# Hybrid decoder step: stick-breaking heads ahead of the delta rule, and paged attention of the samples in plain float32 on four column groups

## The chip, the cores and the metric

The kernel runs on one core of one Trainium2 chip. The metric is device microseconds of a whole execution; the figure given for a kernel is the median of its runs. Engines: PE (TensorE), DVE (VectorE), ACT (ScalarE), POOL (GpSimd), SP (which issues most DMAs).

## The reference

One layer of a decoder trunk runs for two groups with the same weights: a prompt of 512 tokens, and 8 samples of 4 new tokens each, which have 512 past tokens in a paged key and value cache (4 pages of 128 tokens per sample). Per layer:

```
h = RMSNorm(x);  one projection h @ w_in gives  sq,sk,sv | gq,gk,gv,ga,gb,gz
SB, 8 heads of 128:   z = q.k * scale + bias;  w = sigmoid(z) * prod over later keys of (1 - sigmoid(z'));  o = w @ v
                      (samples: keys and values are the cached pages and the 4 new rows)
GDN, 8 heads of 128:  short causal convolution (4 taps) and silu on q|k|v, then the gated delta rule
                      S <- g*S + k (v - w S)^T  in chunks of 64 tokens, o = q S + ...;  o = RMSNorm(o) * silu(gz)
x += [o_SB | o_GDN] @ w_out
x += w_xo @ cross attention(RMSNorm(x), 256 memory tokens, 4 heads, QK-norm, softmax)
x += SwiGLU(RMSNorm(x))
```

Besides the two outputs, new keys and values, the GDN states (8 samples x 8 heads x 128 x 128, and the prompt's), the convolution's last rows and the memory's keys and values are returned. All of it is float32.

## The kernel before, in words

Activations lie transposed, features on the 128 partitions and the 544 tokens (512 + 32) in two halves of 272. A dense product of float32 accuracy is made of three fp32r products of high and low parts: `products` issues six matmuls (`wh,ah`, `wh,al`, `wl,ah`, two halves each) for one 128x128 block of weights. `project` makes one head's 128 output features out of 16 such blocks; `w_in` alone is 64 projects, `mix_out` 16 more. Weights arrive as 512 KB tiles and are split by ACT (`wh`) and DVE (`wl`).

Everything that is not a dense product is *side work*, written as Python generators: a head (`sb_head`, `gdn_head`), the samples' part of four heads (`sb_sample`, `gdn_sample`), `conv_state`. The class `Side` holds two queues of them, `hi` for heads and `lo` for samples. After each group of six dense matmuls `products` calls `tick(0.68)`, which adds 0.68 times `ratio` to a credit; while there is credit, the next generator that is not pausing is run to its next `yield cost, latency`. The cost is taken off the credit, and the generator pauses until the planned time has moved on by the latency. `limits` tells how many of each queue may be open at once. `finish` and `drain` force steps whatever the credit. All of it happens when the program is built: what comes out is a fixed order on every engine, which a scheduler of the tile framework may still move a little. So costs, latencies, ratio and queue order decide what stands beside what on PE.

The order of the stages is: load of x with the first two projections (GDN's q and k of head 0), raw v, constants, then eight GDN heads at ratio 0.8, with `gdn_sample` of four heads each put in the low queue after heads 3 and 7, then `conv_state`; eight SB heads at ratio 2, with `sb_sample` after heads 3 and 7; eight gate heads (`gate_head`, projecting gz); `w_out`; cross attention; SwiGLU. In the trace GDN heads go from about 52 to 480 us, SB heads to about 900, gate heads to about 1093, `w_out` to about 1330, cross attention to about 1480, SwiGLU to the end.

What the samples do on PE: `sample_logits` takes one unit (a sample, two pages or two heads: a 128x512 tile), transposes its four 128x128 blocks (`transposes`, L970), splits the result into high and low parts (`parts`, ACT L666 and DVE L667), and makes four products of 128x256 against a window `win` (L684, L685) that holds the queries of one sample at its own columns and zeros elsewhere, so that all samples add into one PSUM tile (L709). `sample_values` splits pages of values in the same way and makes, for each page, two products (high and low) with 32 rows out (L760); four samples' results are copied side by side into `os`. The cross attention of samples already takes unsplit pages of values (`split=False`, L1509). `gdn_sample` ends with the new states: for each head and four samples one product with K = 32 rows (L1256), then DVE adds it to the old state times a decay, and DMA takes it back. `invert` transposes a triangular inverse by way of DRAM (`scr` to `T`), after which L915 uses it. On PE a plain float32 matmul shows in the trace as two entries.

Of the kernel before, what the change touches and what calls it, by code (L numbers as in the profile page):

```python
# [15 lines left out]
P = 128  # L16
# [7 lines left out]
NB = 8  # L24
# [51 lines left out]
def build_consts(c):  # L76
# [11 lines left out]
    sel(c.cm, [[1, P]], -1, -1, ALU.is_ge, 0.0)  # L88
    c.neg = ones("neg", [P, P], 0.0, pool=pb)
# [15 lines left out]
    def blk(t, fill=0.0, inner=4):  # L105
        sel(t, [[-4, 32], [0, inner]], 1, 0, ALU.is_ge, fill)
        sel(t, [[4, 32], [0, inner]], -1, 3, ALU.is_ge, fill)
# [7 lines left out]
    c.cm4 = ones("cm4", [P, P], pool=pb)  # L115
    blk(c.cm4)
    sel(c.cm4, [[1, P]], -1, -1, ALU.is_ge, 0.0)
# [4 lines left out]

    c.selw = ones("selz", [P, 192], 0.0, pool=c.pc)
    c.selz = c.selw[:, 64:128]
    for part in range(2):
        sel(c.selz, [[-64, 2], [8, 8], [-1, 4]], 1, -56 - 4 * part, ALU.not_equal, 1.0)

    c.selv = ones("selv", [P, 64], 0.0, pool=c.pc)
    for part in range(2):
        sel(c.selv, [[-4, 4], [-32, 4], [-1, 4]], 1, -16 * part, ALU.not_equal, 1.0)  # L130
# [248 lines left out]
def first_projections(c):  # L379

    nc = c.nc
    w = [[None] * 4 for _ in range(2)]

    def wload(q):
        for i in range(2):
            w[i][q] = weights(c, c.w_in, q * 4, 4, 3072 + i * 1024, eng=nc.scalar if q + i == 0 else None)
# [94 lines left out]
def sb_project(c, h, acts, rstd):  # L481
    nc = c.nc
    raw = []
    for i in range(3):
        ps = project(c, c.w_in, 0, i * 1024 + h * P, acts)
# [99 lines left out]
def sb_sample(c, g):  # L585

    nc = c.nc
    q, k, v = (x[:, g * 4 : g * 4 + 4, :].rearrange("p h t -> p (h t)") for x in c.sbs)
    ps = c.aux()
    for i, x in enumerate((q, k)):  # L590
        sq = c.tt("sq")
        nc.vector.tensor_mul(sq[:, :P], x, x)
        nc.tensor.matmul(ps[:, i * P : (i + 1) * P], c.ones, sq[:, :P], start=True, stop=True)
# [36 lines left out]
    for h2 in range(2):  # L630
# [6 lines left out]
        nc.scalar.copy(zt[:, :512], ps)  # L637
        for p in range(PAGES):
            o = p * P + h2 * 64
            nc.tensor.matmul(psz[:, o : o + 64], zt[:, p * P : (p + 1) * P], c.selz, start=True, stop=True)  # L640
        yield 0.9
# [9 lines left out]
    yield 0.1, 6.0  # L651
# [19 lines left out]
def sample_logits(c, q, h0, load, n, ps=None, col=0):  # L671

    nc = c.nc
    nb, win = 2, []
    for b0 in range(0, NB, nb):
        w = c.tp("win")
        nc.gpsimd.memset(w[:, : nb * 192].bitcast(F32), 0.0)
        for b in range(b0, b0 + nb):  # L680
            o = (b - b0) * 192 + (NB - 1 - b) * 8
            d = w[:, o : o + 256].rearrange("p (h x) -> p h x", h=2)
            x = q[:, h0 * 32 : (h0 + 2) * 32].rearrange("p (h b t) -> p h b t", h=2, b=NB)[:, :, b]
            nc.gpsimd.tensor_copy(d[:, :, 0:4], x)  # L684
            nc.gpsimd.tensor_sub(d[:, :, 4:8], x, d[:, :, 0:4].bitcast(F32))  # L685
            win += [[w[:, (b - b0) * 192 + hh * 64 :][:, :P] for hh in range(2)]]
        yield 0.0, 0.3
    first = ps is None
    if first:
        ps = c.aux()  # L690
# [3 lines left out]
    def ahead():  # L694
        if units:
            nxt.append(parts(c, transposes(c, load(*units.pop(0)))))
# [5 lines left out]
    for u in range(NB * n):  # L702
        b, i = divmod(u, n)
        k2 = nxt.pop(0)
        ahead()
        for hh in range(2):
            for j, k in enumerate(k2):
                o = col + i * 256
                nc.tensor.matmul(  # L709
                    ps[:, o : o + 256], win[b][hh], k.rearrange("p (g h k) -> p h g k", g=2, h=2)[:, hh],  # L710
                    start=first and u == 0 and hh == 0 and j == 0,
                    stop=b == NB - 1 and hh == 1 and j == 1, skip_group_check=True,
                )
        yield 0.9, 0.4
# [3 lines left out]
def sample_values(c, w, n, load, split=True):  # L718
# [7 lines left out]
    for i in range(0, n, 2):  # L726
        t = (c.tp if split else c.tt)("win")
        for j in range(2):
            x = w[:, (i + j) * P : (i + j + 1) * P].rearrange("p (h b t) -> p b h t", h=4, b=NB)
            d = t[:, j * 256 : (j + 1) * 256].rearrange("p (b u h t) -> p b u h t", b=NB, u=2, h=4)  # L730
            nc.scalar.copy(d[:, :, 0], x)
            if split:
                nc.vector.tensor_sub(d[:, :, 1], x, d[:, :, 0].bitcast(F32))
            else:
                nc.gpsimd.memset(d[:, :, 1], 0.0)
        win.append(t)
    yield 0.1
    pso = c.aux()
    units = [(b, i) for b in range(NB) for i in range(n)]
    nxt = []  # L740

    def ahead():
        if units:
            v = load(*units.pop(0))
            nxt.append(parts(c, v) if split else [v])

    ahead()
    ahead()
    ahead()
    yield 0.0  # L750
    for half in range(2):
        o = c.tt("os")
        for b4 in range(4):
            b = half * 4 + b4
            ps = c.aux()
            for i in range(n):
                vs = nxt.pop(0)
                for j, v in enumerate(vs):
                    x = (i % 2) * 256 + b * 32
                    nc.tensor.matmul(ps[:32], win[i // 2][:, x : x + 32], v, start=i == 0 and j == 0, stop=i == n - 1 and j == len(vs) - 1)  # L760
                ahead()
                yield 0.45, 0.4
            nc.scalar.copy(o[b4 * 32 : b4 * 32 + 32, :512], ps[:32])
# [4 lines left out]
        yield 0.9  # L768
# [95 lines left out]
def invert16(c, gt):  # L864
# [33 lines left out]
    yield 0.0, 6  # L898
# [248 lines left out]
def gdn_sample(c, g):  # L1147
# [66 lines left out]
    nc.vector.tensor_copy(qk[:, : 2 * P], pss[:, : 2 * P])  # L1214
    ps = transposes(c, qk, 2)
# [19 lines left out]
    nc.vector.tensor_scalar(on[:, :P], on[:, :P], f, None, ALU.mult)  # L1235
    ps = transposes(c, on, 1)
    o = c.tt("o")
    nc.scalar.activation(o[:, :P], ps[:, :P], AF.Identity, scale=c.g_out)
    nc.sync.dma_start(c.oT[8 + g * 4 : 12 + g * 4, :, NP:].rearrange("h p t -> p h t"), o[:, :P].rearrange("p (h t) -> p h t", h=4))
    yield 0.4  # L1240
# [8 lines left out]
    for hh in range(4):  # L1249
        h = g * 4 + hh  # L1250
        rows = slice(hh * 32, (hh + 1) * 32)
        for w in range(2):
            s = v3(c.load("s1"))
            nc.sync.dma_start(s, c.state[0, w * 4 : w * 4 + 4, h].rearrange("b k d -> k b d"))
            ps = c.aux()
            nc.tensor.matmul(  # L1256
                ps, kn[rows, :], ex[w][rows].rearrange("p b d -> p (b d)"),
                start=True, stop=True, tile_position=(hh * 32, 0),
            )
            for b in range(4):  # L1260
                o = g * 32 + hh * 8 + w * 4 + b
                nc.vector.scalar_tensor_tensor(s[:, b, :], s[:, b, :], c.gend_s[:, o : o + 1], ps[:, b * P : (b + 1) * P], ALU.mult, ALU.add)
            nc.sync.dma_start(c.o_gs_s[0, w * 4 : w * 4 + 4, h].rearrange("b k d -> k b d"), s)
            yield 0.9
# [40 lines left out]
def memory(c):  # L1305
# [22 lines left out]
    for i in range(2):  # L1328
        tiles = [[c.tp("mact") for _ in range(2)] for _ in range(4)]
        acts = [[x[:, k % 2 * 256 : k % 2 * 256 + 256] for x in tiles[k // 2]] for k in range(8)]  # L1330
        for k4 in range(2):
            for a in range(2):
                t = load(i * 2 + k4, a)
                nc.vector.tensor_scalar(t, t, rr[a], None, ALU.mult)
                yield 0.0, 2.0
# [60 lines left out]
def cross_head(c, h, q, out, scale):  # L1396
# [9 lines left out]
    for a2 in range(2):  # L1406
# [5 lines left out]
        yield 0.9, 2.0 * a2  # L1412
# [23 lines left out]
def cross_sample(c, qs, outs, scale, tiles):  # L1436
# [27 lines left out]
    for h2 in range(2):  # L1464
# [13 lines left out]
        ps = yield from sample_logits(c, f, h2 * 2, load, 1, ps if h2 else None, h2 * 256)  # L1478
# [4 lines left out]
    nc.scalar.copy(z[:, :512], ps)  # L1483
    yield 0.0, 1.5
    ps = c.aux()
    for h2 in range(2):
        nc.tensor.matmul(ps[:, :256], c.selw[:, 64 - h2 * 64 :][:, :P], z[:, h2 * 256 : h2 * 256 + 256], start=h2 == 0, stop=h2 == 1)
# [740 lines left out]
def kern(ctx: ExitStack, tc: tile.TileContext, *args, stop=99):  # L2228
# [28 lines left out]
    with tc.tile_pool(name="pb", bufs=1) as pb:  # L2257
# [5 lines left out]
        c.raws = pb.tile([P, 24, 8, 7], F32, name="raws")  # L2263
        c.convp = pb.tile([P, 3, 24], F32, name="convp")
        raws = [gdn_raw(c, i * 8, ps, rstd) for i, ps in enumerate(done)]
        raws.append(gdn_raw(c, 16, project(c, c.w_in, 0, 5120, acts), rstd))
        build_consts(c)
        wc = load_cols(c, "convw", [c.conv_w[0].rearrange("j (m p) -> (j m) p", p=P)], c.pc)
        c.wc = wc.rearrange("p (j m) -> p m j", m=24)
        conv_history(c)  # L2270
# [16 lines left out]
        heads = []  # L2287
        for h in range(8):
            if h > 1:
                side.finish(heads[h - 2], 4)  # L2290
            if h > 2:
                side.finish(heads[h - 3])
            qkv = gdn_project(c, h, acts, rstd) if h else [gdn_conv(c, i * 8, raw) for i, raw in enumerate(raws)]
            if h == 0:
                gates(c, acts, rstd)
            heads.append(side.put(gdn_head(c, h, qkv)))
            if h % 4 == 3:
                side.put(gdn_sample(c, h // 4), True)
        side.put(conv_state(c), True)
        side.limits, side.ratio = (2, 1), 2  # L2300
        for h in range(8):
# [81 lines left out]
```

## Time and profile before

| | us |
|---|---|
| median of 3 runs | 2929.99 (2929.43 to 2930.38) |
| the profiled execution | 2926.94 |
| its span (first to last instruction) | 2925.2 |
| PE busy | 2852.4 |
| mean granted clock of PE | 0.996 |

The profile is of one execution. A row of operations reads: line, engine, operation, output <- inputs, tile (rows*columns of the PE array that the weights take), shape, type, count; behind it the busy time, the mean length of one in ns, and the idle time of the engine ahead of it with what ended it. Matmuls overlap in the pipeline, so the mean length is more than the distance from one start to the next; what a matmul costs is read from starts in the timeline. The waits of an engine are listed by what it waited for. Rows of windows give the length, PE's busy time with its count, the granted clock, the share of DMA and GB/s.

### The profile page before, as it was taken

How to read it: one execution, taken by the hardware profiler on the slowest of the kernel's cores; microseconds unless marked ns; L12 is line 12 of the kernel's file. 1: busy time of each engine (PE TensorE's matmuls, PEld its weight loads, DVE VectorE, ACT ScalarE, POOL GpSimd, SP SyncE). 2: the span in 40 equal slices, each digit the busy share in tenths (PEclk: the TensorE clock that was granted, in tenths of full speed). 3: DMA queues.
4: the chain of work that ended last, by engine and by line, in shares of the span. 5: the costliest groups of instructions: out<-in, count | busy, mean ns of one | idle time of the engine just before them, and what ended most of it. 6: DMA issues, size and time to landing. Idle time of an engine off the chain costs nothing. (4 is left out here: it accounts for less than half of the span.)

```text
span 2925.2 us, 57002 instructions
## 1 busy us (share of the span) xinstructions
PE 2852.4 (98%) x22146; PEld 2762.6 (94%) x22146; DVE 2104.0 (72%) x3320; ACT 1489.1 (51%) x2836; POOL 739.1 (25%) x923
## 2 busy tenths in 40 slices
PE   8999999999999999999989999999999999999998
PEld 7999999889889989999889999999999999999998
DVE  5776775655565565536678888888888887888886
ACT  5544443445555564424654444444444446555675
POOL 3211213312212200003242343333433334221200
PEclk9999999999999999999999999999999999999999
DMA  7323223454463585532544555555455549876653
GB/s 222 92 76 93 79 83 90 132 151 119 131 184 98 177 255 175 149 110 91 166 141 125 173 165 158 155 161 170 146 155 176 154 137 266 262 205 193 196 170 95
DMA packets 633558, 444.39 MB, mean 152 GB/s; under 512 B 36203, under 2 KB 559800, under 8 KB 633288
## 3 DMA queue, kind: packets, MB, share of 16 engines
q1 hardware_dynamic: 601464, 386.31, 44.8%
q0 software_dynamic: 22176, 42.90, 4.8%
q10 hardware_dynamic: 9648, 11.54, 1.1%
q8 instruction: 174, 2.85, 0.4%
q14 instruction: 96, 0.79, 0.1%
HBM read 360.07 MB, written 80.58 MB: 151 GB/s over the span
## 5 line engine op out<-in xcount | busy, mean ns | idle before, releaser
L2030 PE MATMUL gu<-pr,wh 128*128 128x272 f32 x4944 | 672.8, 289 | 7.1 <-ACT pr L1659 3.3
L2030 PEld LDWEIGHTS gu<-pr,wh 128*128 128x128 f32 x4944 | 640.8, 189 | 8.9 <-ACT pr L1659 3.9
L215 PE MATMUL mm<-ah,wh 128*128 128x272 f32 (+1 forms) x2464 | 539.2, 299 | 3.9 <-ACT ah L331 2.8
L215 PE MATMUL mm<-al,wh 128*128 128x272 f32 (+1 forms) x2464 | 525.0, 292 | 0.7 <-DVE al L246 0.7
L215 PE MATMUL mm<-ah,wl 128*128 128x272 f32 (+1 forms) x2464 | 516.5, 290 | 0.1
L1910 PE MATMUL bank<-pr,wh 128*128 128x272 f32 x2464 | 466.1, 289 | 1.1 <-ACT bank L1938 1.1
L215 PEld LDWEIGHTS mm<-ah,wh 128*128 128x128 f32 (+1 forms) x2464 | 392.7, 189 | 26.9 <-issue 8.5
L215 PEld LDWEIGHTS mm<-al,wh 128*128 128x128 f32 (+1 forms) x2464 | 390.3, 189 | 5.4 <-issue 2.0
L215 PEld LDWEIGHTS mm<-ah,wl 128*128 128x128 f32 (+1 forms) x2464 | 387.0, 189 | 2.5 <-DVE wl L204 0.5
L1910 PEld LDWEIGHTS bank<-pr,wh 128*128 128x128 f32 x2464 | 386.3, 189 | 3.1 <-ACT bank L1938 2.9
L204 DVE TENSOR_TENSOR wl<-wr,wh 128x512 fp32r<-128x512 f32 (+1 forms) x340 | 244.6, 724 | 183.2 <-ACT wh L203 174.6
L203 ACT CAST wh<-wr 128x512 fp32r<-128x512 f32 (+1 forms) x340 | 208.3, 615 | 316.4 <-PE mm L215 275.2
L2030 PE MATMUL gu<-pr,wl 128*128 128x272 f32 x2472 | 362.0, 289 | 2.0 <-issue 1.8
L1910 PE MATMUL bank<-pr,wl 128*128 128x272 f32 x1232 | 355.0, 288 | 0.0
L2030 PEld LDWEIGHTS gu<-pr,wl 128*128 128x128 f32 x2472 | 330.4, 189 | 2.4 <-issue 2.0
L1808 DVE TENSOR_TENSOR wl<-sum,wh 128x1024 fp32r<-128x1024 f32 x172 | 221.0, 1285 | 74.9 <-ACT wh L1804 74.9
L1910 PEld LDWEIGHTS bank<-pr,wl 128*128 128x128 f32 x1232 | 232.3, 189 | 0.0
L1804 ACT CAST wh<-sum 128x1024 fp32r<-128x1024 f32 x172 | 180.3, 1048 | 78.2 <-PE gu L2030 41.8
L1808 DVE TENSOR_TENSOR wl<-raw,wh 128x1024 fp32r<-128x1024 f32 x133 | 204.0, 1535 | 15.3 <-ACT wh L1804 13.5
L1804 ACT CAST wh<-raw 128x1024 fp32r<-128x1024 f32 x133 | 140.0, 1052 | 101.2 <-PE gu L2030 95.1
L2095 POOL DMA_DIRECT2D pr<-hT x154 | 81.8, 548 | 255.1 <-PE bank L1910 225.2
L1797 DVE TENSOR_TENSOR sum<-raw,sum 128x1024 f32<-128x1024 f32 x86 | 136.4, 1586 | 0.4
(537 smaller groups left out, 4411.2 us busy)
## 6 DMA issues: line engine op xcount, KB each, us to landing
raw<-in_w_gate_up SPq DMA_DIRECT2D x176, 512.0 KB
wr<-in_w_in SPq DMA_DIRECT2D x108, 512.0 KB
raw<-in_w_down SPq DMA_DIRECT2D x176, 256.0 KB
hT<-hs SPq DMA_DIRECT2D x154, 272.0 KB
pr<-hT POOLq DMA_DIRECT2D x154, 272.0 KB, 6.8
page<-in_cache_sb_k SPq DMA_DIRECT2D x128, 128.0 KB
page<-in_cache_sb_v SPq DMA_DIRECT2D x64, 256.0 KB
wr<-in_w_out SPq DMA_DIRECT2D x32, 512.0 KB
```

The costliest lines, as they stand in the source:

```text
L203: nc.scalar.copy(hi[:, :m, :n], raw[:, k : k + m, :n])
L204: nc.vector.tensor_sub(lo[:, :m, :n], raw[:, k : k + m, :n], hi[:, :m, :n].bitcast(F32))
L215: c.nc.tensor.matmul(ps[:n, h, :HT], l[:, :n], r[:, h * HT : (h + 1) * HT], start=first and i == 0, stop=last and i == 2,)
L1797: self.f.c.nc.vector.tensor_sub(self.a[q], self.a[x], self.a[y])
L1804: self.f.c.nc.scalar.copy(self.hi[q], self.left(q))
L1808: self.f.c.nc.vector.tensor_sub(self.lo[q], self.left(q), self.hi[q].bitcast(F32))
L1910: self.c.nc.tensor.matmul(self.c.bank[bank][:, o], t[x][:, s, i * P : (i + 1) * P], pairs[i].op[q][r], start=new and not (i or n), stop=se ...
L2030: self.c.nc.tensor.matmul(bank, w[:, i * P : (i + 1) * P], self.pairs[i].op[q][r], start=start and n == 0, stop=n == 23, skip_group_check= ...
L2095: self.c.nc.gpsimd.dma_start(t, self.hT[2 * g + pair, :, max(0, 2 * n - 1) + k])
```

## The change

The order of the stages is now: load of x with SB's q and k of head 0; eight SB heads; the gates `gates()`; eight GDN heads; eight gate heads. Ratio is 0.65 for SB and GDN and 2 for gate heads, limits are (2, 1) throughout, and the low queue holds `sb_sample` 0 and 1, `gdn_sample` 0 and 1, `conv_state`. The constants of the delta rule are made after SB head 5. A gate head's product with the GDN output waits in a list until that head is done.

In `sample_logits` the transposed unit is only copied (`kT`), and four plain float32 products of 32 rows out and 128 columns go to the four column groups (one per block of the unit). In `sample_values` pages are used as they are loaded, four samples in four column groups. The logits' re-ordering uses two transposes instead of products with `selz`. In `gdn_sample` two heads' new states are made together, in two row groups, before DVE takes them up. Some yields are new or have longer latencies.

```
 def sample_logits(c, q, h0, load, n, ps=None, col=0):
-        w = c.tp("win") ...                       # windows with high and low parts of q, two samples each
+    w = c.tt("win")
+    nc.gpsimd.memset(w[:, :512], 0.0)
+    for b in range(NB): nc.gpsimd.tensor_copy(win[:, b, :, b * 4 : b * 4 + 4], x)
+    yield 0.0, 3.0
...
-            nxt.append(parts(c, transposes(c, load(*units.pop(0)))))
+            pt = transposes(c, load(*units.pop(0)))
+            k = c.tt("kT")
+            nc.scalar.copy(k[:, :512], pt)
...
-        for hh in range(2):
-            for j, k in enumerate(k2):
-                nc.tensor.matmul(ps[:, o : o + 256], win[b][hh], k..., ...)
-        yield 0.9, 0.4
+        for x in range(4):
+            nc.tensor.matmul(
+                ps[x * 32 : x * 32 + 32, o : o + P], win[:, b, x % 2, :], k[:, x * P : (x + 1) * P],
+                ..., tile_position=(0, x * 32),
+            )
+        yield 0.7, 0.4
 def sample_values(c, w, n, load):
-            nxt.append(parts(c, v) if split else [v])
+    todo = [(half * 4 + b, i) for half in range(2) for i in range(n) for b in range(4)]
+    for _ in range(6): ahead()                    # six pages ahead instead of three
+    yield 0.1, 1.5
...
-                for j, v in enumerate(vs):
-                    nc.tensor.matmul(ps[:32], win[i // 2][:, x : x + 32], v, ...)
-                yield 0.45, 0.4
+            for b in range(4):
+                nc.tensor.matmul(
+                    ps[b * 32 : b * 32 + 32], win[i // 2][:, x : x + 32], nxt[b], ..., tile_position=(0, b * 32),
+                )
+            yield 0.9, 1.0
 def sb_sample(c, g):
+    yield 0.0, 2.0                                # after sq, now one product of 256 columns
-        for p in range(PAGES):
-            nc.tensor.matmul(psz[:, o : o + 64], zt[:, p * P : (p + 1) * P], c.selz, start=True, stop=True)
-        yield 0.9
+        yield 0.0, 1.0
+        for i in range(2):
+            nc.tensor.transpose(out, zt[:, i * P : (i + 1) * P], c.ident)
+        yield 0.25
-    yield 0.1, 6.0
+    yield 0.1, 9.0                                # after run
 invert:       -    yield 0.0, 6     +    yield 0.0, 8       # after the load of T
 gdn_sample:   +    yield 0.0, 1.0 (after qk)   +    yield 0.0, 3.0 (after on)
-    for hh in range(4): for w in range(2): load s; matmul; 4 x DVE; store; yield 0.9
+    for h2 in range(2): for w in range(2): load 2 s; 2 matmuls (row groups hh * 32); 8 x DVE; 2 stores; yield 1.2, 2.0
 memory:       -    yield 0.0, 2.0   +    yield 0.0, 4.0
 cross_head:   -    yield 0.9, 2.0 * a2   +    yield 0.9, 3.5 * a2
 kern:
+        side.limits, side.ratio = (2, 1), 0.65
+        for h in range(8): ... sb_head ...; after h 5 gdn_consts; after h 6 conv_history; after h 3, 7 sb_sample
+        gates(c, acts, rstd)
+        for h in range(8): ... gdn_head ...; after h 3, 7 gdn_sample
+        side.put(conv_state(c), True)
+        side.ratio = 2
+        for h in range(8): ... gate_head ...
```

Three places of the new order. First the values of the pages on PE: before, in `sb_sample` of heads 4 to 7, two products (high and low part of one page) between the six dense ones of a block (`mm`).

```order
L760 MATMUL aux<-part,win 32x512 x2
L215 MATMUL mm<-ah,wh 128x272 x2
L215 MATMUL mm<-al,wh 128x272 x2
L215 MATMUL mm<-ah,wl 128x272 x2
L760 MATMUL aux<-part,win 32x512 x2
```

After, at the start of the values of heads 0 to 3, beside an SB head's own transposes and products (L968, L513):

```order
L752 MATMUL aux<-page,win 32x512 x4
L218 MATMUL mm<-ah,wh 128x272 x2
L218 MATMUL mm<-al,wh 128x272 x2
L218 MATMUL mm<-ah,wl 128x272 x2
L513 MATMUL aux<-part,onesr 128x512 x2
L752 MATMUL aux<-page,win 32x512 x3
L968 MATMUL aux<-ident,raw 128x128 x4
L752 MATMUL aux<-page,win 32x512
L218 MATMUL mm<-ah,wh 128x272 x2
L218 MATMUL mm<-al,wh 128x272 x2
L218 MATMUL mm<-ah,wl 128x272 x2
L752 MATMUL aux<-page,win 32x512 x2
```

A group of four that the code issues together does not stay together: dense products stand between its parts. Over the whole program the 64 products stand in 37 places: 22 of one, 9 of two, 3 of three, 2 of four, 1 of seven.

Second the logits on PE, after: each unit's four products stand in one row, next to the transposes of the unit behind it.

```order
L711 MATMUL aux<-kT,win 32x128 x4
L968 MATMUL aux<-ident,page 128x128 x4
L551 MATMUL aux<-z,sfx 128x128
L711 MATMUL aux<-kT,win 32x128 x4
L968 MATMUL aux<-ident,page 128x128 x4
L218 MATMUL mm<-al,wh 128x272
```

Before, the same place had `L709 MATMUL aux<-part,win 128x256 x4` (or split in two) and the same transposes. Four products of a unit stay four, of half the columns and a quarter of the rows out.

Third POOL in the delta rule, before: `gdn_sample`'s convolution (sqk, sctmp) stands ahead of a head's qd and gt.

```order
L1159 TENSOR_TENSOR sctmp<-raws,convw 128x128
L1161 TENSOR_TENSOR sqk<-sqk,sctmp 128x128
L1065 TENSOR_TENSOR qd<-qd,cv 128x512
L1159 TENSOR_TENSOR sctmp<-raws,convw 128x128
L1161 TENSOR_TENSOR sqk<-sqk,sctmp 128x128
L1159 TENSOR_TENSOR sctmp<-raws,convw 128x128
L1161 TENSOR_TENSOR sqk<-sqk,sctmp 128x128
L1159 TENSOR_TENSOR sctmp<-raws,convw 128x128
L1078 TENSOR_TENSOR gt<-cumrow,sm 128x512
```

After, with the second `gdn_sample`:

```order
L1159 TENSOR_TENSOR sqk<-sqk,sctmp 128x128
L1157 TENSOR_TENSOR sctmp<-raws,convw 128x128
L1063 TENSOR_TENSOR qd<-qd,cv 128x512
L1159 TENSOR_TENSOR sqk<-sqk,sctmp 128x128
L1157 TENSOR_TENSOR sctmp<-raws,convw 128x128
L1159 TENSOR_TENSOR sqk<-sqk,sctmp 128x128
L1076 TENSOR_TENSOR gt<-cumrow,sm 128x512
```

The convolution stays ahead of gt, and the same stands once more with the first `gdn_sample`. On PE the new states (L1256 before, L1259 after) go from 12 places of one and 2 of two to 6 places of two and 1 of four.

More of the change, by code (lines that the diff above doesn't have):

```diff
@@ L121, in build_consts @@
     blk(c.sel4, inner=1)
[L123 to L130, printed above, removed]
     c.id16 = ones("id16", [32, 256], pool=c.pc)
@@ new lines, in sample_values @@
+    for _ in range(6):
+        ahead()
+    yield 0.1, 1.5
+    pso = c.aux()
+    for half in range(2):
+        ps = c.aux()
+        for i in range(n):
+            for b in range(4):
+                x = ((i % 2) * NB + half * 4 + b) * 32
+                nc.tensor.matmul(
+                    ps[b * 32 : b * 32 + 32], win[i // 2][:, x : x + 32], nxt[b], start=i == 0, stop=i == n - 1,
+                    skip_group_check=True, tile_position=(0, b * 32),
+                )
+            del nxt[:4]
+            for _ in range(4):
+                ahead()
+            yield 0.9, 1.0
+        o = c.tt("os")
+        nc.scalar.copy(o[:, :512], ps)
@@ L1486, in cross_sample @@
     for h2 in range(2):
-        nc.tensor.matmul(ps[:, :256], c.selw[:, 64 - h2 * 64 :][:, :P], z[:, h2 * 256 : h2 * 256 + 256], start=h2 == 0, stop=h2 == 1)
+        for k in range(2):
+            nc.tensor.matmul(
+                ps[h2 * 64 : h2 * 64 + 64, k * P : (k + 1) * P], c.ident[:, k * 64 : k * 64 + 64], z[:, h2 * P : (h2 + 1) * P],
+                start=k == 0, stop=k == 1, skip_group_check=True, tile_position=(0, h2 * 64),
+            )
     e = softmax(c, ps, 1)
```

222 lines of the change are left out of this document (107 added, 115 removed).

## The prediction

> **What bounds the kernel now.** I read the page's first part, then the chain of waits, then PE's waits, and last the timeline around the operations that change.
>
> ```profile
> span 2925.2 us, 57002 instructions
> PE 2852.4 (98%) x22146; PEld 2762.6 (94%) x22146; DVE 2104.0 (72%) x3320; ACT 1489.1 (51%) x2836; POOL 739.1 (25%) x923
> 1600.00:2400.00 800.00, 800.00 (x6394) 1.00 0.52 158
> ```
>
> PE is busy for 98% of the span; what is left is 2925.2 - 2852.4 = 73 us. The last row is a window in the SwiGLU part: no idle time at all, 6394 matmuls in 800 us, so a dense slot is 125 ns. Everything after about 1480 us is like this and is not touched. So the time can change in two ways only: PE gets more or less work before 1480 us, or some of the 73 us of waits goes or grows. What the change takes from DVE, ACT or POOL counts only where PE waits for them. The profiled execution took 2926.94 us (1.7 us outside the span), 3.0 us under the median of the runs, 2929.99. I sum against the 2926.94 and add 3 at the end.
>
> PE's waits, by what they were for (us in total, times, longest):
>
> ```profile
> PE aux L312 <- POOL lev L60: 6.4, 1, 6.4
> PE aux L942 <- DVE X L938: 4.1, 1, 4.1
> PE aux L915 <- DMA T<-scr: 3.5, 3, 1.5
> PE aux L1418 <- DVE e L1392: 3.4, 4, 1.6
> PE aux L593 <- DVE sq L592: 2.2, 2, 1.1
> PE aux L709 <- POOL win L685: 2.2, 1, 2.2
> PE aux L654 <- POOL run L650: 1.7, 1, 1.7
> PE aux L970 <- DVE mem L1334: 1.7, 1, 1.7
> PE aux L760 <- DVE part L667: 1.6, 2, 1.0
> PE aux L709 <- POOL win L684: 1.5, 1, 1.5
> PE aux L970 <- DVE qk L1214: 1.0, 1, 1.0
> PE aux L709 <- DVE part L667: 0.9, 2, 0.6
> ```
>
> All but the first two (and L1418) are small waits inside side work: heads or samples whose next step came up on PE before its input was there.
>
> **The change on PE, part by part.** The dense matmuls are the same in number. What changes are the samples' small products, and with them how often PE goes from a full 128x128 product to one in a 32-wide tile and back. Four places of the timeline price that:
>
> ```profile
> 1459.73 1.07 PE L1509 MATMUL aux<-xv,win 128*32 128x512 f32 x8
> 1460.73 0.40 PE L1589 MATMUL mm<-xh,wl 128*128 128x272 f32 x1
> 1460.96 0.29 PE L1589 MATMUL mm<-xh,wh 128*128 128x272 f32 x1
> ...
> 1461.59 0.29 PE L1589 MATMUL mm<-xh,wl 128*128 128x272 f32 x1
> 1461.81 1.18 PE L1509 MATMUL aux<-xv,win 128*32 128x512 f32 x4
> 1462.92 0.40 PE L1589 MATMUL mm<-xh,wh 128*128 128x272 f32 x1
> 1463.15 0.29 PE L1589 MATMUL mm<-xl,wh 128*128 128x272 f32 x1
> 530.34 1.12 PE L1256 MATMUL aux<-ex,kns 32*128 32x512 f32 x2
> 531.39 0.66 PE L970 MATMUL aux<-ident,raw 128*128 128x128 f32 x4
> 840.41 0.62 PE L760 MATMUL aux<-part,win 128*32 128x512 f32 x2
> 840.88 0.41 PE L215 MATMUL mm<-ah,wh 128*128 128x272 f32 x2
> 720.66 0.72 PE L709 MATMUL aux<-part,win 128*128 128x256 f32 x4
> 721.21 0.60 PE L970 MATMUL aux<-ident,page 128*128 128x128 f32 x4
> 721.57 0.73 PE L709 MATMUL aux<-part,win 128*128 128x256 f32 x4
> ```
>
> Starts are to be read here, not lengths. L1509 is the cross attention's value product, which already is plain float32 on column groups; a matmul there shows as two entries (x8 is four matmuls). Four matmuls hold PE from 1459.73 to 1460.73, 1.00 us; two of them from 1461.81 to 1462.92, 1.11 us; and L1256, one matmul in a row group, from 530.34 to 531.39, 1.05 us. So one, two or four cost the same: matmuls in different groups overlap, and a lone one has the whole price. Beside it, the dense slot ahead is 0.22 (1461.59 to 1461.81) and the one behind 0.23 us (1460.73 to 1460.96) instead of 0.125: 0.2 us more. A run of one to four such matmuls costs about 1.2 us (1.2 to 1.3).
>
> *Values of the pages.* Before: 128 products L760 (64 high, 64 low parts) in fp32r on one column group; two take 0.47 us (840.41 to 840.88), with no longer neighbours, so 128 x 0.235 = 30.1 us. After: 64 plain matmuls, meant as 16 quads. But the new order on PE has them scattered, dense products between them: 22 lone ones, 9 pairs, 3 threes, 2 fours and one of seven, that is 38 prices of 1.2 us = 45.6. That is +15 us (at 1.3: +19; if lone ones were cheaper than the rows say, say 1.0: +8). The Trainium skill, TensorEngine Tiling (Array Packing), section Key Properties, says that changing the tiling mode drains TensorE; the trace agrees, by the 0.2 us of longer neighbours. Its section Theoretical Speedup gives up to four times for 32 columns; by that alone the values would come to a quarter of a plain float32 serial run, and that is my second rival.
>
> *Logits of the pages.* Before, four products of a unit take 0.55 us (720.66 to 721.21), 80 units: 44 us. After, a unit is one run of four plain matmuls of 128 columns in four column groups, and the order keeps them together (77 runs of four among 79). A pass of 128 plain columns costs 0.09 us (721.21 to 721.57 holds four transposes); a run of 512 columns costs 1.2, of which two passes of 4 x 0.09 are 0.72 to 0.85, so the switch is 0.35 to 0.5; two passes of 128 and the switch make 0.53 to 0.68. I take 0.54 as these runs mostly border on transposes and on each other: -1 us (-2 to +10). That the shorter matmul is worth nothing here is the point: the switch eats it.
>
> *New states (L1256).* Before: 16 matmuls, 12 alone and 2 pairs on the same row group, so 12 x 1.2 + 2 x 2.1 = 18.6. After: six pairs and one four in different row groups. No row shows row groups side by side. Nearest is L1509 (column groups, two for the price of one): 7 x 1.2 = 8.4, -10; if they go one after the other, 6 x 2.1 + 3.9 = 16.5, -2. I take -8.
>
> *Small ones.* The matmuls with selz give way to 8 transposes:
>
> ```profile
> L640 PE MATMUL aux<-selz,zt 128*128 128x64 f32 x32 | 4.3, 278 | 0.8 <-ACT zt L637 0.8
> ```
>
> -2.7 (32 entries between 0.09, a plain pass of 128 columns as above, and 4.3/32 = 0.13 are 3.5; the 8 transposes are 0.8). The cross values come in 2 runs of eight instead of four runs: -1.5. sq, xz and the rest cost nothing on PE. The sum of work: 15 - 1 - 8 - 2.7 - 1.5 = +2 us, between about -8 and +16.
>
> *DVE, ACT, POOL.* DVE loses the low parts of pages (144 subtractions of 128x512), ACT their 64 copies. PE waits for them only in the two rows with "part" (2.5 us), so that is all that their time is worth; it stands in the sum below.
>
> **The change in the waits.** New pauses (the yields) stand between producing and using for T, e, sq, mem, run, qk; win is made at another place, part is gone. Rows T 3.5, e 3.4, sq 2.2, win 2.2 and 1.5, run 1.7, mem 1.7, part 1.6 and 0.9, qk 1.0 add up to 19.7 us. A pause takes the wait away only if other work is ready: dense products are, while projections last, and side work is now spread at 0.65 of dense work instead of 0.8 and then 2, and all through the first 54 of 57 projects. I take 15 of the 19.7 as gone (8 to 20). Named work that hides them: the dense products of the same project, and behind them the other head's steps, of which a pause lets one more go ahead; where a project's dense products are used up, the wait stays.
>
> A stall or a run of idle work also costs clock:
>
> ```profile
> 461.90:465.30 3.40, 0.00 (x0) 0.99 0.11 36
> 465.30:472.10 6.80, 6.26 (x32) 0.50 0.13 28
> 557.40:561.00 3.60, 3.60 (x17) 0.53 0.92 280
> 957.00:960.50 3.50, 3.50 (x20) 0.54 0.62 194
> 1363.00:1366.50 3.50, 3.14 (x15) 0.52 0.00 0
> ```
>
> The third column from the right of each row is the granted clock: after the empty 3.4 us at 461.9 PE ran at half speed for 6.8 us (a loss of 3.4), and three other windows lost 1.7 each. The Trainium skill, TensorE: Matmul & The Clock Gate, Part 1, says that a window of some 3.4 us of low activity halves the clock; the rows agree. As GDN heads and samples' ends get dense work between them, I take two of the three short ones as gone: -3 (0 to -5).
>
> **What stays or comes.** The 4.1 us (row L942) have this cause:
>
> ```profile
> 457.75 0.78 POOL L1161 TENSOR_TENSOR sqk<-sqk,sctmp 128x128 f32<-128x128 f32 x1
> 462.16 1.04 POOL L1078 TENSOR_TENSOR gt<-cumrow,sm 128x512 f32<-128x512 f32 x1
> 463.23 0.69 DVE L1079 TENSOR_TENSOR gt<-gt,aux 128x512 f32<-128x512 f32 x1 [5.02 <-POOL gt L1078]
> 465.84 1.11 PE L942 MATMUL aux<-TT,X 64*64 64x64 f32 x8 [4.14 <-DVE X L938]
> ```
>
> On POOL the convolution of gdn_sample stands in a row ahead of the head's gt; DVE waits 5.0 us for gt, and X, which PE needs, stands behind it on DVE. The new order has the same row of convolution operations ahead of a gt twice, with head 3 or 4 and with head 7. So it stays once (0), and a second one may come: 4.1 + 3.4 = 7.5, taken at half, +4 (0 to +8). The page loads are as many bytes; the values wait now directly on a page instead of on parts of it, and each quad takes four pages; no page wait shows in the trace, 0 to +4. The start (L312, 6.4) is the same order on PE.
>
> **Sum.** +2 - 15 - 3 + 4 = -12. 2926.9 - 12 + 3 = 2918 us.
>
> **Rivals.**
> 1. *The overlap pays as meant*: lone matmuls cost less than the rows' 1.2 because PE goes on with dense weights during them, or runs close up; the values then come to 16 x 1.2 = 19.2, -11 instead of +15, and the sum is -38, or -25 if half of it comes: 2905 to 2892, in the middle 2898. For it: 1.00 us for four. Against: the order scatters them and one alone cost 1.05.
> 2. *Nothing gained*: with logits at the upper end (0.68) the work is 15 + 10 - 8 - 4 = +13, the waits are -14: 2929, as before. For it: the 0.68 is within the rows, and the waits are many small ones, of which each names only the input that came last, so the next one may be hardly earlier.
> 3. *Slower*: lone matmuls and switches. There are about 117 runs in tile mode from pages now, none before at a switch's price. At 1.3 for values and 0.68 for logits the work is +19 + 10 - 2 - 4 = +23; the waits are -12 and a second stall at POOL +7.5: +18, 2948. It decides, with my other terms, from a price of about 1.5 for a value run (38 x 1.5 - 30.1 = +27 against -27 of the rest); or from logits at 0.68 with half of the waits left. For it: 22 lone ones. Against: two, three and four cost the same in the rows, so no dearer kind of run shows.
>
> **Chances.** Forecast (between -20 and -6) 0.42; rival 1 (under -20) 0.16; rival 2 (-6 to +6) 0.20; rival 3 (above +6) 0.22. A difference of 0.2% (5.9 us) is about what a measurement can tell. So faster 0.58, same 0.20, slower 0.22. The range leaves out the far ends of rivals 1 and 3, about 0.1 each: 2896 (-34) to 2940 (+10). The forecast alone would be 2910 to 2924.
>
> **What would show it.** Right: PE's idle falls from 73 to some 60 us and the rows T, sq, win, part and mem are gone or under 1 us; the page values stand as entries of two with about 1.05 us to the next start; a unit of logits takes as long as before; two new-state matmuls in different row groups show 1.05 us for both. Wrong: a lone value matmul followed within 0.6 us by a dense one (rival 1); a wait of PE on page or kT, two L942-like stalls (rival 3); PE busy above 2870 us.

## The result and the profile after

| | before | after |
|---|---|---|
| median | 2929.71 us (2926.26 to 2930.38, 4 runs) | 2949.07 us (2947.4 to 2952.93, 4 runs) |
| profiled execution's span | 2925.2 us | 2947.8 us |
| mean granted clock | 0.996 | 0.992 |

The ratio is 1.007, with an interval of 1.0053 to 1.0088: some 20 us slower, where -12 was forecast. That is the number of the third rival (2948), but not, as it turned out, its mechanism.

```profile
span 2947.8 us, 57119 instructions
PE 2864.5 (97%) x22442; PEld 2725.5 (92%) x22442; DVE 2009.0 (68%) x3168; ACT 1447.9 (49%) x2760; POOL 721.7 (24%) x858
```

PE is busy for 12.1 us more and idle for 10.5 us more. Where, a table of windows by stage tells: the first six rows are of the kernel before, then six of the kernel after. The stages are the start; heads and gate heads up to 60 projects of dense products; the bulk of `w_out`; the rest up to the end of `w_xq`; cross attention with `w_xo`; SwiGLU.

```profile
0.00:60.00 60.00, 48.31 (x337) 1.00 0.80 244
60.00:1135.40 1075.40, 1042.70 (x7915) 0.99 0.44 127
1135.40:1301.60 166.20, 166.18 (x1339) 1.00 0.48 142
1301.60:1406.20 104.60, 101.48 (x762) 0.98 0.29 87
1406.20:1482.70 76.50, 70.80 (x519) 1.00 0.56 185
1482.70:2925.20 1442.50, 1422.93 (x11286) 1.00 0.57 170
```

```profile
0.00:60.00 60.00, 47.77 (x330) 1.00 0.79 240
60.00:1130.50 1070.50, 1042.27 (x8099) 0.99 0.44 126
1130.50:1303.30 172.80, 172.17 (x1391) 1.00 0.47 140
1303.30:1403.90 100.60, 98.28 (x754) 1.00 0.30 90
1403.90:1501.70 97.80, 78.06 (x596) 0.86 0.46 144
1501.70:2947.80 1446.10, 1425.98 (x11286) 1.00 0.57 170
```

Up to the end of `w_xq`, that is in all the stages that I had thought about, the kernel is 2.3 us faster (1403.9 against 1406.2). The loss is in one stage of under 100 us: cross attention takes 97.8 instead of 76.5 us, +21.3, with 14.0 us more idle time (19.7 against 5.7) and a granted clock of 0.86 instead of 1.00. SwiGLU's +3.6 is not explained: in the profiles of this study, none of which changes that stage, it took 1441 to 1446 us.

The timeline of PE in that stage (before, the samples' part stood between dense products L1589 to its end):

```profile
1455.30 0.28 PE L1598 MATMUL mm<-xh,wl 128*128 128x272 f32 x1
1457.12 0.63 PE L968 MATMUL aux<-ident,xk 128*128 128x128 f32 x4 [1.54 <-DMA xk<-in_cache_mem_k]
1458.58 0.63 PE L711 MATMUL aux<-kT,win 128*32 128x128 f32 x8 [0.82 <-ACT kT L699]
1461.18 1.08 PE L968 MATMUL aux<-ident,xk 128*128 128x128 f32 x4 [1.98 <-DMA xk<-in_cache_mem_k]
1463.04 0.65 PE L711 MATMUL aux<-kT,win 128*32 128x128 f32 x8 [0.77 <-ACT kT L699]
...
1473.13 0.66 PE L968 MATMUL aux<-ident,e 128*128 128x128 f32 x2 [2.13 <-DVE e L1396]
1475.45 3.64 PE L1518 MATMUL aux<-xv,win 128*32 128x512 f32 x16 [1.65 <-POOL acc L270]
1479.90 1.06 PE L1530 MATMUL aux<-selv,os 128*128 128x16 f32 x8 [0.81 <-ACT os L1526]
```

At 1455.3 the 192 dense products of the first half of `w_xo` are used up. Four units of logits, the softmax and both value steps of the samples are left, and the second half may only start when they are done. For 30 us PE has nothing else: a load, a transposition, a copy, four small products, in a chain. What the loads themselves waited for shows in the waits of SP's DMA queue in this stage, before (first row) and after (the other two):

```profile
SPq L1473 <- PE aux L970: 8.1, 3, 7.2
```

```profile
SPq L1477 <- PE aux L711: 13.9, 4, 6.6
SPq L1459 <- PE aux L711: 8.9, 3, 5.7
```

L1477 is the load of a key block `xk`. Before, it waited for transposes (L970), the readers of older key blocks. Now it waits for L711, the reader of `kT`: both tiles come from one ring (`c.tt`, which in this stage is the 16 places tagged "ah"). The split parts had come from the other ring (`c.tp`, tagged "al"). So the change makes a unit take two places of one ring, the ring from which the next units are loaded.

And the clock:

```profile
1455.00:1485.00 30.00, 16.88 (x105) 0.66 0.44 132
1458.00:1479.00 21.00, 11.15 (x70) 0.52 0.42 120
```

From 1458 to 1479 us PE was busy in half of the time, with small products, at about half clock. Here and below, *lost clock* is one minus the granted clock, summed over windows of 1 us: 13.7 us in this stage, 0 before. Of the 13.7, 10.2 lie in the stretch without dense products and 3.4 at 1414 to 1421 us, behind earlier waits for `kT` (2.69 us) and for a key block (1.83).

### The profile page after: what moved, and what is told of

It is laid out like the page before. It is cut to its first block, busy times and chain, and to the rows that moved or that the text cites. A ratio compares the mean times of both kernels' runs of the same rounds, so it can differ in the third digit from the quotient of the medians.

```text
span 2947.8 us, 57119 instructions
## 1 busy us (share of the span) xinstructions
PE 2864.5 (97%) x22442; PEld 2725.5 (92%) x22442; DVE 2009.0 (68%) x3168; ACT 1447.9 (49%) x2760; POOL 721.7 (24%) x858
## 5 line engine op out<-in xcount | busy, mean ns | idle before, releaser
L218 PE MATMUL mm<-ah,wh 128*128 128x272 f32 (+1 forms) x2464 | 546.6, 301 | 6.0 <-ACT ah L334 3.7
L218 PEld LDWEIGHTS mm<-al,wh 128*128 128x128 f32 (+1 forms) x2464 | 388.8, 188 | 12.1 <-issue 9.1
L1817 DVE TENSOR_TENSOR wl<-raw,wh 128x1024 fp32r<-128x1024 f32 x133 | 202.6, 1524 | 15.7 <-ACT wh L1813 13.7
```

The costliest lines, as they stand in the source:

```text
L218: c.nc.tensor.matmul(ps[:n, h, :HT], l[:, :n], r[:, h * HT : (h + 1) * HT], start=first and i == 0, stop=last and i == 2,)
L1817: self.f.c.nc.vector.tensor_sub(self.lo[q], self.left(q), self.hi[q].bitcast(F32))
```

## The experiments

**The ring of kT.** Theory 1 is the shared ring, its rival that plain float32 in 32-wide tiles, or the pauses, cost the 20 us. First the changed kernel with one edit, named e_kt:

```
-            k = c.tt("kT")
+            k = c.tp("kT")[:, :512].bitcast(F32) if n == 1 else c.tt("kT")[:, :512]     # n == 1: cross attention
```

> The changed kernel, only the transposed key blocks kT of the cross attention's samples taken from the other ring of tiles (the one that the split parts came from before). Theory 1 (shared ring): kT takes the places of the next key loads xk, these start late, the last units and both value steps are left over when the dense products of the stage are used up, and PE runs them alone at half clock. Then the order of this kernel, with the logits done at dense product 134 of 192 instead of after 192, should give back 12 to 19 us: 2930 to 2937, with the stage from the end of w_xq to the first SwiGLU product at 79 to 86 us instead of 98, no wait for xk above 2.5 us, and at most one half-clock stretch of 3.4 us there. Theory 2 (the 20 us are the price of plain float32 in 32-wide tiles and of the new pauses): unchanged, 2945 to 2950.

Measured: 2928.61 us, ratio to the kernel before 1.0003 (0.9993 to 1.0013). Next, e_before_x is the kernel before with nothing but the new cross logits, in the ring that the change gave them:

> The kernel before, only the cross attention's samples with the new logits (plain float32, kT from the ring of the key loads, four column groups, new re-ordering). Theory 1: the whole loss of that stage comes with this edit alone, whatever the stages ahead are: +17 to +21 us, 2947 to 2951, with about 10 us of full clock lost between the end of w_xq and SwiGLU. Theory 2 (the loss needs the new order of stages or the new pauses of the heads): 2928 to 2934.

Measured: 2951.27 us, ratio 1.008 (1.0063 to 1.0097), with 18.8 us of lost clock in the stage, where about 10 were expected. Last the two other corners: e_before_x_al takes kT of that kernel from the other ring, and e_before_ring leaves the old split products alone and takes only their parts from the ring of the loads (in short):

```
-    hi, lo = (c.tp("part") for _ in range(2))
+    hi, lo = (c.tt("part")[:, :512].bitcast(F32R) for _ in range(2))                     # cross attention only
```

> The kernel before with the new cross logits (plain float32, four column groups), but kT in the ring where the split parts were. With kT in the ring of the key loads this kernel took 2951.3. If the ring is the cause: 2926 to 2933. If the plain products in 32-wide tiles are: 2945 to 2952.

> The kernel before with its own split products in fp32r, only the two parts of the cross attention's key blocks taken from the ring of the key loads. In the order on PE four units are then left behind dense product 192 of the first half, as in the changed kernel. If the ring is the cause, whatever the products are: 2942 to 2952. If the plain products in 32-wide tiles are: 2926 to 2931.

Measured: 2929.92 us, 1.0007 (0.9998 to 1.0017), and 2954.81 us, 1.0093 (1.0076 to 1.011). The cross stage in windows, in the order e_kt, e_before_x, e_before_x_al, e_before_ring:

```profile
1402.80:1483.10 80.30, 72.64 (x593) 0.98 0.54 174
```
```profile
1406.80:1506.20 99.40, 79.64 (x585) 0.81 0.43 141
```
```profile
1405.90:1485.00 79.10, 71.73 (x584) 0.96 0.54 176
```
```profile
1403.40:1507.50 104.10, 83.80 (x516) 0.84 0.42 134
```

| time of the kernel, us | tiles in the other ring | tiles in the ring of the loads |
|---|---|---|
| old products (high and low parts), old order | 2927 to 2930 (before) | 2954.8 |
| new products, old order | 2929.9 | 2951.3 |
| new products, everything else new | 2928.6 | 2949.1 (after) |

It is the ring, whichever products use it: from one column to the other of each row only the ring changes. The sizes are somewhat off the expectations, e_kt 1.4 us under its range and e_before_ring 2.8 over. Everything else in the change together comes to nothing (e_kt).

How the ring acts shows in the order on PE, which is fixed when the program is built. In the traces the last product of the samples' logits stands behind all 192 dense products of the first half in the three kernels of the right column, and behind 110 (before), 134 (e_kt) and 124 (e_before_x_al) of them in the left column. It is not the summed wait of the loads: in e_kt the key loads wait no shorter in total than in the changed kernel, but again for the transposes (now L968), and for the readers of `kT` only 1.8 us instead of 13.9.

```profile
SPq L1477 <- PE aux L968: 13.9, 6, 7.8
```

How the ring leads the build to that order was not looked into.

**The half clock.** e_fill adds 56 plain products in the stretch without dense work, behind the logits of the last units and around the softmax. With them the samples' cross attention is not the reference's; its time is what is read here.

```
+        if n == 1 and col and u > 2:
+            for _ in range(8):
+                nc.tensor.matmul(ps[:, 384:512], c.ident, c.ident, start=True, stop=True, ...)
...                                             # and twice eight more, around the transposes of e
```

> The changed kernel with 56 plain products of 128x128 by 128 columns (112 entries of about 0.11 us, 12 us of PE work at full clock) added to the samples' part of the cross attention, in the stretch after the dense products are used up; nothing reads them. If the half clock in that stretch (10.2 us of full clock lost) comes from PE having too little to do there, more work shortens it: the lost clock falls to 2 to 5 us, and the time comes out at 2938 to 2949, no longer in spite of 12 us more work. If the half clock comes from anything else, the time is 2953 to 2961.

Measured: 2952.72 us, 1.0087 (1.007 to 1.0104), between the two expectations. In the stage:

```profile
1400.90:1504.00 103.10, 88.76 (x705) 0.95 0.43 137
```

Lost clock fell from 13.7 to 5.1 us and idle time from 19.7 to 14.3, and the stage took 5.3 us more. The stretch without dense products alone, first in the changed kernel and then with the filler:

```profile
1455.30:1486.60 31.30, 17.49 (x109) 0.67 0.41 123
1455.06:1487.40 32.34, 24.24 (x203) 1.00 0.33 99
```

Here the half clock is gone altogether, so it does come from PE having too little to do; whether busy time counts or how much of the array is used, this run does not tell. But the stretch is 1.0 us longer, not shorter: what the clock gave back, the added products took. The other 4.3 us lie ahead of it (2.8, where one group of eight stands) and behind it (1.5, with 1.7 of lost clock). The chain without cover is there in both; this filler bought nothing back.

**Values in fours.** In the changed kernel the pause after each four value products goes from 1 to 8 (e_quads); then 15 of the 16 groups stand together in the order on PE, 17 places instead of 37. e_both has this and the repaired ring.

```
-            yield 0.9, 1.0
+            yield 0.9, 8.0
```

> The changed kernel, only the pause after each four value products in the samples' paged attention lengthened from 1 to 8, so that in the order on PE 15 of the 16 groups of four stay together (17 places instead of 37). If a run costs 1.18 us whatever it holds up to four, 20 places fewer are 20 x 1.18 = -23.6 us on PE: 2925. Rival: the lone ones were partly hidden in other waits or the longer pause brings new waits: -5 to -12, 2937 to 2944.

> Both edits (kT from the other ring, pause of 8 after each four values). If the two causes are independent, the gains add up: -15 - 23.6, 2910, 20 us under the kernel before. If they are one and the same (one stretch of time counted twice): 2925 to 2930.

Measured: e_quads 2925.11 us, 0.9998 of before (0.9988 to 1.0007), so 0.7% under the kernel after; e_both 2909.07, 0.9933 (0.9916 to 0.995). e_quads is 21 us (by the ratios) to 24 us (by the medians) under the changed kernel, where 23.6 were expected; in its trace the values hold PE for 16.9 us in 17 places instead of 37.3 in 37. e_both is 40 us under it, against 20 and 21 for the two alone by the ratios: the gains add up.

**Logits by two units.** e_pairs goes on from e_both: in `sb_sample` two units' products are issued together, with a pause of 4 behind them.

```
-    for u in range(NB * n):
+    for u0 in range(0, NB * n, n):
+        for u in range(u0, u0 + n):
...
-        ahead()
-        yield 0.7, 0.4
+        for _ in range(n): ahead()
+        yield 0.7 * n, 4.0 if n == 2 else 0.4
```

> The two repairs (kT in the other ring, values in groups of four), and the paged logits taken two units at a time: 30 places of eight products in the order on PE, 51 places in all instead of 80. If the switch into and out of 32-wide tiles costs about 0.33 us a place (a run of four took 0.36 us, of which two passes of 128 columns are about 0.2, and the neighbours are 0.13 to 0.2 longer), 29 places fewer are 9.6 us: 2899 to 2901 against 2909. Rival: the pairs need two units ready, PE waits for the second kT instead: 2906 to 2912.

Measured: 2891.17 us, 0.9875 (0.9858 to 0.9891): 18 us under e_both, where 9.6 were expected. A row of its timeline with two units in one place:

```profile
270.38 0.65 PE L712 MATMUL aux<-kT,win 128*32 128x128 f32 x16
270.95 0.91 PE L533 MATMUL aux<-hat,raw 128*128 128x384 f32 x2
```

Eight products hold PE for 0.57 us where two fours hold it for 2 x 0.36 (median), and one pair of longer neighbours falls away. Up to the end of `w_xq` the two profiles differ by 17.3 us (1381.4 and 1364.1): the lost clock is 5.1 us less and the idle time 4.1 less, so about 8 are the places, near the 9.6 expected; by the starts, the paged logits hold PE for 4.0 us less and their neighbours are 4.3 us shorter. The other 9 were not foreseen and their cause was not tested.

**Order and pauses.** e_order has the new order of stages with all products as before, and all pauses but one: T's stays at 8 instead of 6, though its expectation says that all pauses are as before. e_nopause is e_kt without the eight new pauses listed here; those inside the new products stay. e_order_p is e_order with the eight. e_oldorder is e_pairs with the old order of stages.

```
e_nopause:   -    yield 0.0, 2.0 (sq), 0.0, 1.0 (zt, qk), 0.0, 3.0 (on)
             -    run 9.0, T 8, memory 4.0, cross_head 3.5      +    6.0, 6, 2.0, 2.0
e_oldorder:  kern, first_projections, build_consts as before
```

> The new order of stages alone (stick-breaking heads first, one ratio of 0.65, gates between), with the samples' attention, cross attention, new states and all pauses as before. The cross attention's order on PE is as before, so its stage should take 76 us as before. Theory 1 (the waits that I expected to go are replaced by other small waits, whichever order the stages have): 2924 to 2932, no change. Theory 2 (the new order has the gain of 10 to 15 us in waits, and only the new small products spend it): 2913 to 2920.

> The changed kernel with kT of the cross attention in the other ring, and without the new pauses (sq, zt, qk, on gone; run, T, memory and cross heads back to their old latencies). Against the kernel with the pauses and that ring (2928.6): theory 1 (the pauses only move which input is late): 2925 to 2933; theory 2 (the pauses do take away some 15 us of waits, and something else of the same size was added): 2938 to 2945.

> The new order of stages with the new pauses (sq, zt, run, T, qk, on, memory, cross heads), and the samples' small products and new states as before. The new order alone took 2932.9. Theory 1 (the pauses take 15 to 24 us of waits and half clock whatever the products are): 2909 to 2918, so that the new small products with kT repaired cost 10 to 20 us on top of it. Theory 2 (the pauses are worth that much only beside the new products, whose inputs they make wait less): 2924 to 2933.

> The old order of stages (delta rule first, ratios 0.8 and 2) with everything else of the fastest kernel so far (pauses, plain products, kT in the other ring, values in fours, logits two units at a time; that one took 2891.2). The new order alone cost 5 to 6 us against the kernel before. Theory 1 (the order costs the same here): 2884 to 2888. Theory 2 (the order is what gives the new products their cover): 2896 to 2910.

| | median, us | ratio to before | idle, lost clock, 60 us to end of w_xq |
|---|---|---|---|
| e_order | 2932.87 | 1.0017 (1.0008 to 1.0027) | 35.5, 8.5 |
| e_order_p | 2931.72 | 1.0015 (1.0005 to 1.0025) | 32.4, 6.8 |
| e_nopause | 2952.2 | 1.0074 (1.0054 to 1.0094) | 45.9, 15.3 |
| e_kt (pauses) | 2928.61 | 1.0003 (0.9993 to 1.0013) | 28.5, 8.5 |
| e_oldorder | 2937.53 | 1.0031 (1.0021 to 1.0041) | 48.4, 20.4 |
| e_pairs (new order) | 2891.17 | 0.9875 (0.9858 to 0.9891) | 29.0, 3.4 |

Each idle time is length less busy time of one window; for e_nopause, e_kt, e_oldorder and e_pairs:

```profile
60.00:1432.00 1372.00, 1326.06 (x10246) 0.99 0.42 123
```
```profile
60.00:1402.80 1342.80, 1314.35 (x10238) 0.99 0.43 125
```
```profile
60.00:1408.80 1348.80, 1300.38 (x10233) 0.98 0.43 126
```
```profile
60.00:1364.10 1304.10, 1275.07 (x10238) 1.00 0.44 129
```

Two of these miss both of their ranges: e_nopause is 7 us slower than its slower theory, and e_oldorder 28 us. e_order is 0.9 us over the range of its theory 1, e_order_p inside that of its theory 2.

The new order (with T's pause) costs 5 us. With the old products the pauses come to 1 us, which is within the noise, but that is a balance: up to the end of `w_xq` e_order_p is 8.3 us faster than e_order (1401.6 and 1409.9 us), and its cross attention, first e_order and then e_order_p, takes 7.9 us longer:

```profile
1409.90:1487.50 77.60, 72.28 (x517) 0.98 0.55 180
1401.60:1487.10 85.50, 76.39 (x524) 0.96 0.50 163
```

With the new products the pauses are worth 21 us by the ratios and 24 by the medians, all of it ahead of the cross attention. It does not come from fewer places: values and logits stand in 35 and 80 places without the pauses, in 37 and 81 with them.

With the old order, the products and pauses of the fastest kernel leave 19 us more idle time and 17 more lost clock, and it is slower than before. The trace of e_oldorder shows where a large part of this is: between the gate heads and `w_out` PE has no dense product for 36.6 us.

```profile
1062.30:1098.90 36.60, 24.87 (x83) 0.84 0.70 231
```

In it stand half of the page values, whose two runs of sixteen products take 14.4 and 12.7 us, partly in wait of their pages; in e_pairs four products take 1.00 us, and from 60 us to the end of `w_xq` no stretch without a dense product is longer than 5.0 us. That is the same kind of loss as in the cross attention: side work left behind the last dense product of a stage. The rest of the 46 us between e_oldorder and e_pairs was not followed up, and no run moves this stretch alone. So the parts cannot be priced one by one: what a pause or an order is worth depends on which side work it leaves without cover.

## Why the prediction was wrong

- *Values, +15.* Right. A lone one and a pair cost the same, 0.98 us to the next start, and 37 places hold PE for 37.3 us, to which the longer neighbours add 0.2 each (0.09 ahead, 0.105 behind): 44.5 against 30.5, +14.

```profile
336.52 1.05 PE L752 MATMUL aux<-page,win 128*32 128x512 f32 x4
337.50 0.52 PE L218 MATMUL mm<-ah,wh 128*128 128x272 f32 x2
...
338.44 1.05 PE L752 MATMUL aux<-page,win 128*32 128x512 f32 x2
339.42 0.52 PE L218 MATMUL mm<-ah,wh 128*128 128x272 f32 x2
```

- *New states, -8.* Right: row groups do run side by side. A pair in two row groups holds PE for 1.06 us, where a pair in one row group took 1.91 before. Four matmuls, two by two, hold it from 824.38 to 826.29, 1.91 us; all of them 8.3 us, against 16.4 before.

```profile
824.38 1.99 PE L1259 MATMUL aux<-ex,kns 32*128 32x512 f32 x8
826.29 0.52 PE L218 MATMUL mm<-al,wh 128*128 128x272 f32 x2
```

- *Logits, -1, and the sum of the work, +2.* Right: a unit holds PE for 0.36 us and makes its neighbours about 0.17 longer, 0.53 against 0.54 in the forecast. PE's busy time up to the end of `w_xq` went from 1358.7 to 1360.5 us, +1.8; the forecast has +3.5 for these stages (the -1.5 lies in the cross attention), and 1.7 less of lost clock is in the busy time.
- *Waits, -15.* Wrong in the balance. The rows that I named did shrink, from 19.7 to 6.2 us (T and run gone, sq at 2.0 as before). X, which I had kept, went from 4.1 to 0.9. But the idle time of those stages fell only from 47.5 to 43.4, because others came or grew:

```profile
PE aux L1110 <- DVE ve L1106: 4.7, 5, 2.8
PE mm L218 <- ACT ah L334: 3.7, 3, 1.8
PE aux L913 <- DVE TT L956: 3.1, 3, 1.6
PE aux L1166 <- POOL sqk L859: 2.7, 2, 1.5
...
PE mm L218 <- ACT wh L206: 1.9, 2, 1.4
PE aux L792 <- DVE ab L788: 1.7, 1, 1.7
```

I had put new waits at +4, for a second stall at gt; they are some 12 us of many kinds, and none is that one. The two terms together, -15 and +4, were off by 7 us: 4.1 us of idle time went, not 11.
- *Half clock, -3.* In those stages 8.5 us lost before, 6.8 after: -1.7.
- *The cross attention.* This is the step that failed. I priced its new products on PE ("xz and the rest cost nothing", "the cross values come in 2 runs of eight instead of four runs: -1.5") and counted of the parts that fall away only the waits for them. I did not ask which ring of tiles kT comes from, nor who waits for its place: the loads on SP's queue, and behind them the end of a stage that has only so many dense products as cover. In place of -1.5 the stage took +21.3, nearly all of the 22.6 by which the profiles differ. The order on PE had the sign: the logits' last four units behind the last dense product. That the values stand there in 2 runs of eight is not it, for they do so in e_kt too, whose stage is only 3.8 us longer than before.
- *The sum.* Between the forecast of -12 and the +22.6 of the profiles lie 34.6 us: 22.8 in the cross attention, 8.2 in the stages ahead of it (6.9 of waits and 1.3 of half clock) and 3.6 in SwiGLU, which is not explained. PE's idle time, which was to fall from 73 to some 60 us, rose to 83.
- *The rivals.* The first did not come: lone products have the full price. The second, nothing gained, is what the change is without the ring (e_kt, 1.0003): not by dearer logits, but its remark that each wait names only the input that came last fits the waits that came back. The third had the number by chance. The price per place stayed near the 1.2 of the forecast, and its second stall at POOL did not come.
- *The rules that I cited.* The Trainium skill, TensorEngine Tiling (Array Packing), Key Properties, says that changing the tiling mode drains TensorE; the 0.2 us of longer neighbours at each place of values agree. Of what e_quads gave back, some 20 us are the places themselves and some 4 the neighbours. The same page of the Trainium skill, Theoretical Speedup, gives up to four times for 32 columns; that holds for four products that stand together, 1.00 us for four and 0.98 for one (the forecast calls it the second rival; in its list it is the first). The Trainium skill, TensorE: Matmul & The Clock Gate, Part 1, speaks of an idle window of about 3.4 us; the lost clock of every stage summed here is a multiple of 1.7 us within 0.1, that is of 3.4 us at half rate, but the 21 us at 0.52 above were not idle.

## What to carry to other kernels

When a tile changes its type or its life, look up from which ring it comes, who else takes places there, and which load waits for them; then see how much dense work is left as cover at the end of that stage. Read in the order on PE what stands behind the last dense product of a stage: that is exposed time, and there the small products cost their whole chain. Up to four narrow tiles on column groups paid here by the place in the order, not by the product: keep them together, with a pause long enough that all inputs are there.

## What the runs showed of the hardware that was not expected

Two matmuls in different row groups ran side by side, with all 128 columns out, as column groups did: 1.05 us for a lone one, 1.06 for two in different row groups, 1.91 for two in one row group before. The clock fell to half though PE was not idle for more than 2.13 us at a time: 11.15 us of 21 busy, with small products, at a granted clock of 0.52. With products added, 24.24 us busy of 32.34, the same stretch had the full clock.
